# Weight sums for the last down projection moved to GpSimd, in tiles taken from the transfer scratch

## The chip, the cores and the metric

The kernel runs on one core of one Trainium2 chip, as one program from one launch. The metric is the device time of that program in microseconds (us); smaller is better. Engines carry the profile's names: PE is TensorE, PEld its weight loads, DVE is VectorE, ACT is ScalarE, POOL is GpSimd and SP is SyncE, which here only issues transfers. SPq, ACTq and POOLq are the queues from which an engine issues transfers (DMAs).

## What is computed

Two layers of a decoder trunk over 512 positions of width 1024, all float32. A layer is a mixer and a gated MLP, each with a norm ahead of it and a residual sum behind it:

```
for l in range(2):
    h = rmsnorm(x, norm1_g[l]);  p = h @ w_in[l]
    y_rw  = rwkv7_branch(...)        # 8 heads of 64, state recurrence over the positions
    y_ret = retention_branch(...)    # 4 heads, chunks of 128 positions
    y_sg  = sgu_branch(...)          # gated spatial unit, chunks of 128
    gates = sigmoid(gate_logits)
    x = x + (sum over the 3 branches of gates * (y @ w_branch)) @ w_out[l]
    u = rmsnorm(x, norm2_g[l]) @ ffn_w_up[l]         # 1024 -> 2 x 2816
    c = causal convolution of width 3 over the positions of u
    x = x + (silu(gate half of c) * value half of c) @ ffn_w_down[l]   # 2816 -> 1024
return rmsnorm(x, final_g)
```

## The kernel before

All products are made on TensorE in three passes: each operand is split into a rounded part and a remainder (`hi`, `lo`), and `mm3` (L152, the matmul itself at L156) issues three products (hi by lo, hi by hi, lo by hi) of mostly 128 x 128 by 128 x 512. Weights come as 128 x 512 units: `load` issues the transfer from SP into a raw tile `wr`, `part` makes the rounded part on ACT (L139, tiles `wh` or `sh`) and the remainder on DVE (L140, `wl` or `sl`). The program is built twice; the first pass notes the order of the units, the second fetches ahead by that plan (`unit`, `AHEAD`). The order of the instructions on each engine is set when the program is built, by a scheduler that goes by priority (program order, if nothing else is said) and by a modelled time; `keep_in_program_order` pins an instruction behind whatever its engine has traced before it. On the chip each engine then runs its queue strictly in order.

Tiles of 128 x 512 float32 (2 KiB per partition) come from rotating pools: `u` has `NU` = 31, `r` has 16, `f` (while the merges and the MLP run) has 39. A tile is given again when its last reader is done.

One layer runs so. `rwkv`: columns of the projection, `prep` per pair of heads (ends with four masks on POOL, L579 and L580), then `solve`, a triangular solve on DVE that begins with copies of diagonal blocks (L769 on ACT, L771 on POOL), then the recurrence over eight chunks of 64 positions. In the solve and the recurrence, TensorE fills its waits with `fill`: columns of the gates, retention and spatial unit, kept in store by the generator `fillers`. A chunk passes from the state S (L712, L713 on DVE) to XB (L687 on DVE) to U (L701 on ACT) and back, each time with small products at L664. Every second chunk ends with a power operation on POOL (L732). Behind the recurrence come `sgu_v` (power operation L990), and the merges in the order written out in `SEQ`: S stands for a row of retention (power operation L961 on POOL), 0, 2 and 1 for a branch's merge of one column block. A merge fetches its gate (`gth`, L1034, POOL queue), multiplies on DVE (L1037) and adds on POOL or DVE (L1040). Then `wout`, `ffn_up`, and `ffn_down` in the first layer, `last` in the second.

`last` makes the last down projection in a form with fewer products: of each pair of row blocks of the weight it uses four tiles as they are and four sums or differences of them. The sums do not depend on data, and the kernel makes them ahead and puts them into DRAM (`tsum`), from where `last` fetches them like weights (`ts` tiles, SP queue). There are eleven pairs q, each with four loads, four sums and four stores. In the kernel before, all of that is done in the first layer's MLP by `presum`, which is called in `ffn_up` and `ffn_down` where the table `PRE` says so: loads and stores from the POOL queue, sums on DVE (L242 to L245), in tiles of the pools `f` (`fpre`, sixteen tiles) and `u`.

Of the kernel before, what the change touches and what calls it, by code (L numbers as in the profile page):

```python
# [8 lines left out]
F32 = mybir.dt.float32  # L9
# [6 lines left out]
L = 2  # L16
# [3 lines left out]
NFF = 22  # L20
DFF = 2816
RWC, RETC, SGC = 1792, 1536, 1024
NU, NR, NFP = 31, 16, 39
FILL = (36, 2, 1)
KEPT = 6
PRE = {(0, "f", 2): 0, (0, "f", 4): 1, (0, "f", 6): 2, (0, "f", 8): 3, (0, "d", 0): 4, (0, "d", 1): 5, (0, "d", 2): 6, (0, "d", 3): 7,
       (0, "d", 4): 8, (0, "d", 5): 9, (0, "d", 6): 10}
# [24 lines left out]
class Emit:  # L52
    def __init__(self, ctx, tc, a, plan=None):

        self.plan, self.used = plan, []
        self.raws, self.parts, self.nraw, self.npart = [], [], 0, 0
        self.pool, self.fp, self.pin, self.keep, self.turn = None, None, False, False, 4
        self.tc, self.nc, self.a = tc, tc.nc, a
        tp = lambda n, b, **k: ctx.enter_context(tc.tile_pool(name=n, bufs=b, **k))
        self.cp = tp("cp", 1)  # L60
        self.wp = tp("wp", 2)
        self.up = tp("up", NU)
        self.rg = tp("rg", NR)
# [172 lines left out]

    def presum(self, l, stage, m):

        if self.pre:
            q, b = self.pre.pop()  # L240
            V = self.nc.vector
            V.tensor_tensor(b[3], b[3], b[1], op=SUB)  # L242
            V.tensor_tensor(b[1], b[1], b[0], op=SUB)
            V.tensor_tensor(b[0], b[0], b[3], op=ADD)
            V.tensor_tensor(b[2], b[2], b[0], op=SUB)  # L245
            for p, t in zip((7, 5, 6, 4), (b[3], b[1], b[0], b[2])):
                self.tsum[q, p] = self.dp.tile([128, 512], F32, name=self.nm("ts"))
                self.nc.gpsimd.dma_start(self.tsum[q, p], t)
        q = PRE.get((l, stage, m))
        if q is not None:  # L250
            b = self.fpre.pop(0) if stage == "f" else [self.u(n="pre") for _ in range(4)]
            for i, t in enumerate(b):
                self.nc.gpsimd.dma_start(t, self.a["wdt"][0, 2 * q + i // 2][:, i % 2 * 512:i % 2 * 512 + 512])
            self.pre.append((q, b))

# [68 lines left out]
    def run(self):  # L324
        nc, tc, a, V = self.nc, self.tc, self.a, self.nc.vector
        self.con = self.cp.tile([128, NCC], F32, name="con")
        self.pre, self.tsum = [], {}
        self.rst = self.cp.tile([128, 512], F32, name="rst")
# [132 lines left out]
    def rwkv(self, l, nst):  # L461
# [64 lines left out]
        def prep(m):  # L526
# [146 lines left out]
        for c in range(8):  # L673
# [13 lines left out]
            V.tensor_copy(xb, Q[:, 1])  # L687
            self.fill(FILL[2], True)
            Q = self.sm((128, 2, 4, 64)) if c < 7 else None
            for i in (0, 4, 5, 6, 7, 1, 2, 3):  # L690
                for h in range(2):
# [7 lines left out]
                    else:  # L699
                        mm(P1[hv[o], 0, m, :], Y[m][hv[o], c, 64:128], vop(hv[o], m, c))  # L700
            A.copy(U, P1[:, 1])  # L701
            self.fill(FILL[2], True)
            for m, h in mh:
# [339 lines left out]
    def wout(self, l, mg, xd, st):  # L1043
        nc, V = self.nc, self.nc.vector
        out = []
        for m in range(8):
            xi = self.u(n="xi")
            nc.sync.dma_start(xi, xd[m])
            ps = self.acc()
            self.matF(ps, ("wall", l, 70 + m, 0), mg)  # L1050
            V.scalar_tensor_tensor(xi, ps, 0.5, xi, op0=MUL, op1=ADD)
            out.append(xi)
            self.norm_z(st, xi, "n2")
            self.norm_sq(st, xi)
# [3 lines left out]
    def ffn_up(self, l, st, x):  # L1058
# [9 lines left out]
        first = self.firstF(l, (78, 79, 80), st, (3,))  # L1068
        if l == 0:
            self.fpre = [[self.f(n="pre") for _ in range(4)] for _ in range(4)]  # L1070
        for i in range(NFF):
            if l == 0 and i % 2 == 0 and 2 <= i <= 10:
                self.presum(l, "f", i)
            if x and i % 2 == 1 and i < 17:
# [42 lines left out]
    def ffn_down(self, l, act, x, st):  # L1117
# [3 lines left out]
        for m in range(8):  # L1121
# [7 lines left out]
            xd.append(d)  # L1129
            self.presum(l, "d", m)  # L1130
        return x, xd


    def last(self, act):
# [8 lines left out]
        def unit(p, q):  # L1143
            if p > 3:
                return self.unit("tsum", 0, (q, p), 0)
            return self.unit("wdt", 0, 2 * q + (p > 1), 512 * (p == 3))
# [289 lines left out]
```

## Time and profile before

| | |
|---|---|
| time, median of 3 runs | 1703.91 us (1703.56 to 1705.05) |
| the profiled execution's own time | 1701.58 us |
| its span, first to last instruction | 1699.7 us |
| granted TensorE clock | 0.999 |
| TensorE busy | 1687.0 us (99%) |
| VectorE busy | 1233.1 us (73%) |
| ScalarE busy | 799.9 us (47%) |
| GpSimd busy | 240.8 us (14%) |
| moved by DMA | 260.01 MB, 153 GB/s on the mean |

Busy time is the time in which an engine has an instruction in work; TensorE's matmuls overlap each other, so that a matmul of 128 x 512 shows 390 ns. The stretches of the span are, roughly: to 345 us the first layer's heads and recurrence, to 460 its merges, to 510 its output projection, to 865 its MLP (down projection from 755), to 985 the second layer's head preparation, to 1045 its solve, to 1155 its recurrence, to 1303 gating unit and merges, to 1345 the output projection, to about 1595 the up projection, then `last`.

### The profile page before, as it was taken

Reading aid. Unit: us, or ns where it says so; the run is one execution under the profiler, and the core shown is the slowest. Engines: PE = TensorE matmul, PEld = TensorE weight load, DVE = VectorE, ACT = ScalarE, POOL = GpSimd, SP = SyncE. Lnnn points to the kernel's source line nnn. Section 1 sums busy time; section 2 is a strip of 40 time slices with the busy share of each in tenths; the row PEclk is TensorE's granted clock in tenths of the full one; section 3 lists DMA queues with packets and bytes.
Section 4 is the critical chain, followed back from the end, with each engine's and each line's share of the span. In section 5 each row is a group of like instructions: output and inputs, shape, how many; then the busy total and the mean of one; then the engine's idle time right before and its main releaser. Section 6 shows DMA issues by size and latency. Waiting matters only on the chain.

```text
span 1699.7 us, 27885 instructions
## 1 busy us (share of the span) xinstructions
PE 1687.0 (99%) x10214; PEld 1379.7 (81%) x10214; DVE 1233.1 (73%) x2157; ACT 799.9 (47%) x1367; POOL 240.8 (14%) x336
## 2 busy tenths in 40 slices
PE   9999999999999999999999999999999999999998
PEld 7888777888888888888888888777888888887786
DVE  6887746578669887655568888455775698888776
ACT  6563433554355444433355644335542554444565
POOL 2121000003301200003321210000132022110000
PEclk9999999999999999999999999999999999999999
DMA  5236552524544532147743365525254443433774
GB/s 182 87 108 203 177 179 94 181 92 161 189 146 147 194 123 95 63 145 260 255 142 100 97 211 172 180 94 188 85 173 149 155 136 132 130 131 112 241 243 167
DMA packets 147768, 260.01 MB, mean 153 GB/s; under 512 B 19600, under 2 KB 39952, under 8 KB 147632
## 3 DMA queue, kind: packets, MB, share of 16 engines
q1 hardware_dynamic: 122960, 192.87, 35.2%
q0 software_dynamic: 15888, 49.95, 8.7%
q10 hardware_dynamic: 8784, 15.42, 2.6%
q8 instruction: 80, 1.31, 0.3%
q14 instruction: 56, 0.46, 0.1%
HBM read 212.94 MB, written 45.22 MB: 152 GB/s over the span
## 4 chain that ended last, share of the span: by engine, by line
PE 90%; DVE 4%; DMA 3%; issue 1%; ACT 1%; SPq 0%; ACTq 0%; DVEq 0%
PE acc L156 82%; PE sm L156 3%; PE sm L664 2%; DVE wl L140 1%; DMA wr<-wall 1%; PE sm L917 1%; PE sm L571 1%; DMA tr<-bkT 1%; DVE sl L140 0%; PE sm L1022 0%; ACT wh L139 0%; DVE cs L790 0%; DMA wr<-ts 0%; DVE TMP L788 0%; DMA x<-xT 0%
## 5 line engine op out<-in xcount | busy, mean ns | idle before, releaser
L156 PE MATMUL acc<-lo,sh 128*128 128x512 f32 x1108 | 431.8, 390 | 0.5 <-ACT sh L139 0.5
L156 PE MATMUL acc<-hi,sh 128*128 128x512 f32 x1108 | 431.9, 390 | 0.0
L156 PE MATMUL acc<-hi,sl 128*128 128x512 f32 x1108 | 430.3, 390 | 0.2 <-DVE sl L140 0.2
L139 ACT CAST sh<-wr 128x512 fp32r<-128x512 f32 (+1 forms) x375 | 228.3, 615 | 370.3 <-PE acc L156 217.6
L140 DVE TENSOR_TENSOR sl<-wr,sh 128x512 fp32r<-128x512 f32 (+1 forms) x375 | 254.5, 684 | 103.5 <-ACT sh L139 78.3
L140 DVE TENSOR_TENSOR wl<-wr,wh 128x512 fp32r<-128x512 f32 x238 | 166.5, 703 | 144.5 <-ACT wh L139 141.1
L139 ACT CAST wh<-wr 128x512 fp32r<-128x512 f32 x238 | 146.8, 619 | 244.4 <-PE acc L156 160.3
L156 PEld LDWEIGHTS acc<-lo,sh 128*128 128x128 f32 x1108 | 208.0, 188 | 45.0 <-ACT sh L139 1.2
L156 PEld LDWEIGHTS acc<-hi,sl 128*128 128x128 f32 x1108 | 208.0, 188 | 44.1 <-DVE sl L140 0.7
L156 PEld LDWEIGHTS acc<-hi,sh 128*128 128x128 f32 x1108 | 208.0, 188 | 43.1 <-issue 0.3
L156 PE MATMUL acc<-lo,wh 128*128 128x512 f32 x588 | 232.3, 395 | 0.3 <-DVE lo L215 0.2
L156 PE MATMUL acc<-hi,wl 128*128 128x512 f32 x588 | 229.8, 391 | 0.5 <-DVE wl L140 0.5
L156 PE MATMUL acc<-hi,wh 128*128 128x512 f32 x588 | 229.3, 390 | 0.0
L156 PEld LDWEIGHTS acc<-lo,wh 128*128 128x128 f32 x588 | 110.5, 188 | 25.5 <-DVE lo L215 1.5
L156 PEld LDWEIGHTS acc<-hi,wl 128*128 128x128 f32 x588 | 110.4, 188 | 25.4 <-DVE wl L140 1.5
L156 PEld LDWEIGHTS acc<-hi,wh 128*128 128x128 f32 x588 | 110.6, 188 | 22.5 <-issue 0.2
L156 PE MATMUL acc<-ah,sh 128*128 128x512 f32 x352 | 108.4, 389 | 0.0
L1084 ACT ACTIVATE cv<-fu,pc 128x512 f32<-128x512 f32 x88 | 71.6, 816 | 61.1 <-DVE fu L1082 59.8
L1082 DVE TENSOR_TENSOR fu<-acc,rsF 128x512 f32<-128x512 f32 x88 | 60.6, 688 | 39.8 <-PE acc L156 39.7
L156 PE MATMUL acc<-wl,hi 128*128 128x512 f32 x212 | 86.1, 406 | 0.0
L156 PE MATMUL acc<-wh,lo 128*128 128x512 f32 x212 | 82.8, 391 | 0.0
L156 PE MATMUL acc<-wh,hi 128*128 128x512 f32 x212 | 82.7, 390 | 0.0
(359 smaller groups left out, 2426.8 us busy)
## 6 DMA issues: line engine op xcount, KB each, us to landing
wr<-wall SPq DMA_DIRECT2D x488, 256.0 KB, 2.8
gd<-gth ACTq DMA_DIRECT2D x48, 256.0 KB, 3.0
gth<-gd POOLq DMA_DIRECT2D x48, 256.0 KB, 3.5
pre<-wdt POOLq DMA_DIRECT2D x44, 256.0 KB, 5.9
ts<-pre POOLq DMA_DIRECT2D x44, 256.0 KB, 2.8
wr<-ts SPq DMA_DIRECT2D x44, 256.0 KB, 3.9
wr<-wdn SPq DMA_DIRECT2D x40, 256.0 KB, 4.2
wr<-wdt SPq DMA_DIRECT2D x33, 256.0 KB, 3.6
```

What stands on the lines that cost most here:

```text
L139: self.kept(self.nc.scalar.copy(hi[:, :n], raw[:, :n]))
L140: self.kept(self.nc.vector.tensor_tensor(lo[:, :n], raw[:, :n], hi[:, :n], op=SUB))
L156: i = self.nc.tensor.matmul(*x, **y, **kw)
L571: i = T.matmul(pK[hv[1 - h], j, :], bk[hv[h], c, 1, :], x[hv[h], c, :], start=True, stop=True)
L664: po(T.matmul(o, l, r, start=start, stop=True, skip_group_check=True))
L917: po(T.matmul(X[h][:, i, :], lhsT, rhs, start=new[h], stop=stop, skip_group_check=True))
L1082: V.tensor_tensor(u, ps, self.rsF, op=MUL)
L1084: A.activation(t, u, AF.Identity, scale=self.p("cw2", j), bias=self.p("cb", j))
```

## The change

The sums move from DVE in the first layer's MLP to POOL in the second layer's mixer. The generator `sums` holds their steps: four loads into a pool `pp` of four tiles of its own, then an empty step, then four steps of one sum and one store, then an empty one; all of them are POOL instructions and pinned in program order. `presum` now takes a step of it. It is called twice at the end of each `prep` (four times), three times in each chunk (eight), behind each step of the gating unit (nine), ahead of each step of `SEQ` (33) and in each column block of `wout` (eight): 82 calls for 77 steps, in the second layer only (in the first the generator is empty). The room for the tiles comes from the scratch that the program keeps for POOL's transfers, which is set to 4096 bytes per partition (`dynamic_dma_scratch_size`); six tiles are added, four in `pp` and two in `u` (`NU` 33). The tables and the sixteen `fpre` tiles of the first layer go.

```diff
-NU, NR, NFP = 31, 16, 39
+NU, NR, NFP = 33, 16, 39
-PRE = {(0, "f", 2): 0, (0, "f", 4): 1, ... (0, "d", 6): 10}
+RING = 4096
...
+        self.pp = tp("pp", 4)
...
-        src = self.tsum[i] if name == "tsum" else self.a[name][l, i]
+        src = self.tsum[(l, *i)] if name == "tsum" else self.a[name][l, i]
...
-    def presum(self, l, stage, m):
-        if self.pre:
-            q, b = self.pre.pop()
-            V = self.nc.vector
-            V.tensor_tensor(b[3], b[3], b[1], op=SUB)
-            V.tensor_tensor(b[1], b[1], b[0], op=SUB)
-            V.tensor_tensor(b[0], b[0], b[3], op=ADD)
-            V.tensor_tensor(b[2], b[2], b[0], op=SUB)
-            for p, t in zip((7, 5, 6, 4), (b[3], b[1], b[0], b[2])):
-                self.tsum[q, p] = self.dp.tile([128, 512], F32, name=self.nm("ts"))
-                self.nc.gpsimd.dma_start(self.tsum[q, p], t)
-        q = PRE.get((l, stage, m))
-        if q is not None:
-            b = self.fpre.pop(0) if stage == "f" else [self.u(n="pre") for _ in range(4)]
+    def sums(self, l):
+        P, po = self.nc.gpsimd, self.tc.keep_in_program_order
+        for q in range(NFF // 2 if l else 0):
+            b = [self.pp.tile([128, 512], F32, name=self.nm("pre"), tag="pre") for _ in range(4)]
             for i, t in enumerate(b):
-                self.nc.gpsimd.dma_start(t, self.a["wdt"][0, 2 * q + i // 2][...])
-            self.pre.append((q, b))
+                po(P.dma_start(t, self.a["wdt"][l - 1, 2 * q + i // 2][...]))
+            yield
+            yield
+            for p, o, x, op in ((7, 3, 1, SUB), (5, 1, 0, SUB), (6, 0, 3, ADD), (4, 2, 0, SUB)):
+                po(P.tensor_tensor(b[o], b[o], b[x], op=op))
+                self.tsum[l, q, p] = self.dp.tile([128, 512], F32, name=self.nm("ts"))
+                po(P.dma_start(self.tsum[l, q, p], b[o]))
+                yield
+            yield
+
+    def presum(self, n=1):
+        for _ in range(n):
+            next(self.sum, None)
...
# mixer
-            self.filler = self.fillers(l)
+            self.filler, self.sum = self.fillers(l), self.sums(l)
...
             next(step) if step else self.sgu_bias()
+            self.presum()
...
         for step in SEQ.split():
+            self.presum()
...
# rwkv, end of prep
             X.append(x); Y.append(y); BK.append(bk)
+            self.presum(2)
...
# rwkv, in each chunk: behind the tile of P1, behind XB, behind U
+            self.presum()
...
# wout, in each column block
+            self.presum()
...
# ffn_up and ffn_down: the calls of presum and the tiles fpre are gone
...
-        nc = _bacc.Bacc("TRN2", target_bir_lowering=False, num_devices=1)
+        nc = _bacc.Bacc("TRN2", target_bir_lowering=False, num_devices=1, dynamic_dma_scratch_size=RING)
```

More of the change, by code (lines that the diff above doesn't have):

```diff
@@ L235, in trip @@
         return d
-    def presum(self, l, stage, m):
-        if self.pre:
-            q, b = self.pre.pop()
-            V = self.nc.vector
-            V.tensor_tensor(b[3], b[3], b[1], op=SUB)
-            V.tensor_tensor(b[1], b[1], b[0], op=SUB)
-            V.tensor_tensor(b[0], b[0], b[3], op=ADD)
-            V.tensor_tensor(b[2], b[2], b[0], op=SUB)
-            for p, t in zip((7, 5, 6, 4), (b[3], b[1], b[0], b[2])):
-                self.tsum[q, p] = self.dp.tile([128, 512], F32, name=self.nm("ts"))
-                self.nc.gpsimd.dma_start(self.tsum[q, p], t)
-        q = PRE.get((l, stage, m))
-        if q is not None:
-            b = self.fpre.pop(0) if stage == "f" else [self.u(n="pre") for _ in range(4)]
-            for i, t in enumerate(b):
-                self.nc.gpsimd.dma_start(t, self.a["wdt"][0, 2 * q + i // 2][:, i % 2 * 512:i % 2 * 512 + 512])
-            self.pre.append((q, b))
+    def sums(self, l):
+        P, po = self.nc.gpsimd, self.tc.keep_in_program_order
+        for q in range(NFF // 2 if l else 0):
+            b = [self.pp.tile([128, 512], F32, name=self.nm("pre"), tag="pre") for _ in range(4)]
+            for i, t in enumerate(b):
+                po(P.dma_start(t, self.a["wdt"][l - 1, 2 * q + i // 2][:, i % 2 * 512:i % 2 * 512 + 512]))
+            yield
[9 more added lines that the diff above has]
+            next(self.sum, None)
     def norm_new(self):
@@ L326, in run @@
         self.con = self.cp.tile([128, NCC], F32, name="con")
-        self.pre, self.tsum = [], {}
+        self.tsum = {}
         self.rst = self.cp.tile([128, 512], F32, name="rst")
@@ L701, in rwkv @@
             A.copy(U, P1[:, 1])
+            self.presum()
             self.fill(FILL[2], True)
@@ L1052, in wout @@
             out.append(xi)
+            self.presum()
             self.norm_z(st, xi, "n2")
@@ L1068, in ffn_up @@
         first = self.firstF(l, (78, 79, 80), st, (3,))
-        if l == 0:
-            self.fpre = [[self.f(n="pre") for _ in range(4)] for _ in range(4)]
         for i in range(NFF):
-            if l == 0 and i % 2 == 0 and 2 <= i <= 10:
-                self.presum(l, "f", i)
             if x and i % 2 == 1 and i < 17:
@@ L1129, in ffn_down @@
             xd.append(d)
-            self.presum(l, "d", m)
         return x, xd
@@ L1144, in unit @@
             if p > 3:
-                return self.unit("tsum", 0, (q, p), 0)
+                return self.unit("tsum", L - 1, (q, p), 0)
             return self.unit("wdt", 0, 2 * q + (p > 1), 512 * (p == 3))
```

2 lines of the change are left out of this document (removed).

## The prediction

> **What bounds the kernel now.** I read the page first, then busy time by stage (stretches cut by hand), then the waits of TensorE, then the order of time around the moved work.
>
> ```profile
> span 1699.7 us, 27885 instructions
> ```
>
> ```profile
> 510.00:755.00 245.00, 245.00 (x1082) 202.93 (x1082) 197.54 (x311) 114.27 (x179) 15.15 (x29) 1.00 0.37 123
> 755.00:865.00 110.00, 110.00 (x487) 91.10 (x486) 59.04 (x93) 34.15 (x60) 34.23 (x64) 1.00 0.75 251
> ...
> 1045.00:1150.00 105.00, 104.78 (x1559) 81.75 (x1559) 55.61 (x110) 45.19 (x89) 7.15 (x7) 1.00 0.45 143
> ```
>
> The columns of a stretch are its length, then busy time of TensorE, its weight loads, VectorE, ScalarE and GpSimd, the granted clock, the DMA share and GB/s. The first two stretches are the first layer's gated MLP (up, then down projection), where all the removed work stands: TensorE is busy 245.00 of 245.00 us and 110.00 of 110.00. The third is the second layer's recurrence, where the products are small and TensorE is busy 104.78 of 105.00 us. TensorE is the bound in all three, at a full clock, and another engine matters only where it makes TensorE stand still.
>
> ```profile
> PE acc L156 <- DVE sl L140: 0.7, 1, 0.7
> ```
>
> ```profile
> 1175.00:1190.00 15.00, 14.29 (x63) 11.18 (x62) 8.87 (x14) 9.61 (x16) 0.00 (x0) 1.00 0.47 161
> 1550.00:1575.00 25.00, 24.27 (x106) 19.32 (x105) 19.44 (x33) 9.76 (x16) 1.62 (x3) 1.00 0.34 111
> 1575.00:1600.00 25.00, 24.40 (x105) 19.25 (x104) 20.14 (x34) 13.04 (x23) 2.70 (x5) 1.00 0.63 193
> ...
> 1655.00:1690.00 35.00, 34.66 (x153) 28.40 (x152) 28.47 (x52) 19.83 (x41) 2.17 (x4) 1.00 0.56 188
> 1690.00:1700.00 10.00, 2.48 (x11) 1.71 (x10) 2.81 (x7) 3.13 (x9) 0.00 (x0) 0.82 0.29 105
> ```
>
> The first row heads TensorE's waits between 1045 and 1345 us: one wait of 0.7 us. The next four rows are the places behind the first layer where it loses time that more tiles or a freer VectorE could give back: 0.71 + 0.73 + 0.60 + 0.34 = 2.4 us in all. The last row is the tail, 7.5 us without products.
>
> **What is removed.**
>
> ```profile
> L242 DVE TENSOR_TENSOR pre<-pre,pre 128x512 f32<-128x512 f32 x11 | 7.6, 690 | 15.8 <-DMA pre<-wdt 15.8
> ...
> L245 DVE TENSOR_TENSOR pre<-pre,pre 128x512 f32<-128x512 f32 x11 | 7.5, 686 | 0.0
> ```
>
> These are the first and the last of four groups: 44 VectorE operations of some 0.69 us, 30 us of VectorE, and 15.8 us in which it stood waiting for their data. With them 44 loads and 44 stores leave the GpSimd queue of the first layer, 23 MB that made part of the 251 GB/s of its down projection, and the 16 "pre" tiles leave the big pool. All of it lay beside a TensorE without a gap, so it gives back 0. If that cover were missing, at most 30 + 16 us could come back; the two full stretches exclude it.
>
> **What is added.** The same 44 sums on GpSimd, in the second layer between its per-head preparation and its output projection, four tiles at a time: each group is four loads, an empty step, then four times a sum and its store. By the calls in the code that is 4 sums in the preparation, 14 in the recurrence, 6 in the gating unit, 20 in the merges and the output projection.
>
> ```profile
> L248 POOL DMA_DIRECT2D ts<-pre x44 | 23.9, 542 | 194.8 <-DVE pre L242 169.3 <-DVE pre L245 8.4 <-DVE pre L243 6.0
> L253 POOL DMA_DIRECT2D pre<-wdt x44 | 23.4, 539 | 0.0
> L1040 POOL TENSOR_TENSOR gth<-gth,gth 128x512 f32<-128x512 f32 x16 | 21.4, 1338 | 65.0 <-DVE gth L1037 65.0
> ```
>
> A sum of this shape takes GpSimd 1.3 us (the merges' adds), an issue 0.54. So GpSimd gets 44 x 1.3 + 88 x 0.54 = 57 + 48 = 105 us more, over some 400 us; in the recurrence it is busy 7.15 of 105.00 us now. Its own time is no term. What can cost is what stands behind it.
>
> First, the queue. The new instructions are pinned behind whatever GpSimd has traced, so the loads after the last head's masks stand in front of the diagonal copies that start the triangular solve.
>
> ```profile
> 984.20 2.58 POOL L771 COPY cs<-GB 32x1024 f32<-32x1024 f32 x2
> ```
>
> ```profile
> 1037.76 2.28 DVE L794 STREAM_TRANSPOSE cs<-cs 128x512 f32<-128x512 f32 x2
> ```
>
> ```profile
> 1045.38 1.34 PE L808 MATMUL sm<-cs,GB 32*32 32x32 f32 x128
> ```
>
> Four issues put 2.2 us in front of the copies; the solve ends on VectorE at 1040.04 and its first product runs at 1045.38, behind filler products. Slack 5.3 us, price 0; without the fillers it would be 2.2. A sum whose loads have not landed makes GpSimd's small power operations (L732, L961, L990) and the gate loads behind it wait, and VectorE, in order, for those. The landing of the present loads and stores together is 2.3 to 7.7 us, median 4.5, and the code leaves one step between:
>
> ```profile
> DMA to landing us min/median/max: 2.3/4.5/7.7
> ```
>
> ```profile
> ACT sh L139 <- PE acc L156: 37.5, 19, 4.4
> ```
>
> The second view (waits, 1045 to 1345 us) says that ScalarE's weight casts wait mostly for TensorE to free tiles: weights are ready ahead, so a late VectorE does not starve TensorE at once. I take 0.5 us for the gating unit and the merges together, between 0 and 3.8 (five retention rows at 0.75, the overshoot worked out below).
>
> Second, VectorE itself.
>
> ```profile
> 428.29 1.29 POOL L1040 TENSOR_TENSOR gth<-gth,gth 128x512 f32<-128x512 f32 x1 [3.11 <-DVE gth L1037]
> ```
>
> ```profile
> 427.52 1.29 DVE L1037 SCALAR_TENSOR_TENSOR gth<-gth,acc 128x512 f32<-128x512 f32 x2
> ```
>
> ```profile
> 453.47 1.28 POOL L1040 TENSOR_TENSOR gth<-gth,gth 128x512 f32<-128x512 f32 x1 [3.78 <-DVE gth L1037]
> ```
>
> ```profile
> 454.15 1.15 DVE L140 TENSOR_TENSOR sl<-wr,sh 128x512 fp32r<-128x512 f32 x1 [0.77 <-ACT sh L139]
> ```
>
> Beside a GpSimd add that ends at 454.75, the weight remainder L140, which reads two SBUF tiles like the removed sums and at their 0.69 us when undisturbed, takes 1.15 and ends 0.55 behind the add. Two L1037, with one operand in PSUM, run at full speed beside another add (0.65 each). So a VectorE operation with two SBUF operands waits for the end of a running GpSimd sum, 1.29 us at most. That is what the Trainium skill says (SBUF — State Buffer, SBUF: two separate sides): the shared port pair is held exclusively for a whole instruction, by a GpSimd operation or a two-SBUF-input VectorE one, and the loser blocks. It speaks against this change, and by it alone 44 sums would hold VectorE off for up to 57 us. The trace agrees in the rows above. What matters is where VectorE has no 1.3 us to spare, and that is the recurrence.
>
> ```profile
> 1101.29 0.69 DVE L140 TENSOR_TENSOR wl<-wr,wh 128x512 fp32r<-128x512 f32 x1 [3.32 <-ACT wh L139]
> 1101.90 0.42 DVE L712 TENSOR_TENSOR S<-S,sm 128x256 f32<-128x256 f32 x1
> 1102.35 0.42 DVE L713 TENSOR_TENSOR S<-S,F 128x256 f32<-128x256 f32 x1
> ...
> 1105.67 0.68 DVE L140 TENSOR_TENSOR wl<-wr,wh 128x512 fp32r<-128x512 f32 x1
> 1106.27 0.42 DVE L687 COPY XB<-sm 128x256 f32<-128x256 f32 x1
> ```
>
> ```profile
> 1104.18 0.62 PE sm L664 x32
> ...
> 1107.75 1.09 PE sm L664 x64
> ```
>
> The state S is done at 1102.77 and TensorE reads it at 1104.18: slack 1.41 us. XB is done at 1106.69 and read at 1107.75: slack 1.06. One blocked operation costs at most 1.29: S still fits, XB is 0.23 late. Two blocked in a row (L140, then L713 behind a second sum that started beside L712: 1.29 + 1.29 - 0.42 = 2.16) make S 0.75 late. Of the 14 sums here I let 4 meet such a step, at about 0.3 us each, nearer to the single hit of 0.23 than to the double one: +1.2, between 0 and 14 x 0.75 = 10.5. In the preparation TensorE loses nothing measurable now; I take 0 for 4 sums, at most 4 x 0.75 = 3.
>
> **Two more u tiles, four tiles of their own, the smaller scratch.** More u tiles can only give back stalls; I take 0.5 of the 2.4 us. No row shows the scratch. If it is large enough for what is in flight, it costs 0; the row nearest to a queue that holds back is a landing of 4.5 us instead of an issue of 0.54. I take 0, since at most a dozen transfers are issued within one landing.
>
> **Sum.** 0 + 1.2 + 0.5 - 0.5 = +1.2 us. The profiled execution took 1701.58 us (span 1699.7 and 1.9 around it), so it would be 1702.8; the three timed runs have a median of 1703.91, 2.3 above the profiled one, so I forecast 1705.1 there.
>
> **Rivals.**
> *The held port costs the recurrence (slower).* The sums come in bursts right behind a power operation or a landing, and two in a row beat S by 0.75 us. If half of the 14 hit so, it is +5.3 us, with the merges' 3.8 at worst +9.1: 1709 to 1713. It decides from five such hits on. For it: the slack rows; L140 stands before S and XB in order. Against: a sum needs its load, and the loads come only every seventh step.
> *More tiles close the gaps (faster).* All four gaps of 2.4 us vanish and nothing else costs: 1701.5. Reaching beyond 0.2% needs 3.4 us, so a changed order would have to shorten the tail of 7.5 us too. For it: VectorE is 78% busy just before the gaps of 1550 to 1600. Against: the sums are not there in either version.
> *The scratch holds GpSimd's queue (slower).* If transfers wait for earlier ones to land, the MLP's stores "ab" come late, and VectorE overwrites what they read. Eleven pairs at the shortest landing, 2.3 us, make 25 us of VectorE, of which its idle 22 per cent there (25.00 less 19.44, from 1550 on) covers most; a tenth to a quarter left over is +2.5 to +6, 1706 to 1710. For it: these stores are issued from the same queue. Against: the code has eight GpSimd transfers per pair there, which is few.
>
> **How the numbers follow.** About 0.2%, 3.4 us, is what a measurement of this kernel tells from no change. Forecast (stalls of a few tenths, within 0.2%) 0.50; the held port beyond 3.4 us 0.30; the scratch or a less fortunate order of the schedule beyond 3.4 us 0.10; gaps closed beyond 3.4 us 0.10. So faster 0.10, same 0.50, slower 0.40. The range goes from all gaps closed, with half a microsecond of spread, to the held port near its full price: 1701.0 to 1712.0. The forecast's own range is 1702 to 1707.
>
> **What would show it.** Right: both first-layer MLP stretches as full and as long as before; GpSimd some 105 us busier, all between 900 and 1330 us; L140 and L713 of the second recurrence longer or later by up to 1.3 us where a sum runs; 0 to 2 us more idle TensorE in 1045 to 1150. Wrong: a first-layer MLP that gets shorter; TensorE waiting on S, XB or a power operation for over 3.4 us in all; GpSimd issues of far over 0.54 us, which would be the scratch; or the stalls of 1550 to 1600 us gone together with a shorter tail.

## The result, and the profile after

The changed kernel takes 1741.37 us (median of 4 runs, 1740.48 to 1747.11) against 1703.74 us for the kernel before in the same comparison (1703.07 to 1705.05): a ratio of 1.0227, with a 95% interval of 1.0204 to 1.0250, so some 38 us more. The forecast was 1705.1 us with a range to 1712.0. The profiled execution took 1740.48 us.

Of the page of the kernel after, the span, the busy time of the engines, and GpSimd's three new groups (lines behind the recurrence stand seven lower than before: L1037 is now L1044, L1040 L1047, L713 L720, L664 L668; L139, L140 and L156 are unchanged):

```profile
span 1738.7 us, 27762 instructions
...
PE 1702.8 (98%) x10214; PEld 1385.9 (80%) x10214; DVE 1248.0 (72%) x2113; ACT 800.0 (46%) x1367; POOL 302.4 (17%) x380
```

```profile
L247 POOL TENSOR_TENSOR pre<-pre,pre 128x512 f32<-128x512 f32 x44 | 60.6, 1377 | 19.9 <-DMA pre<-wdt 19.1
...
L249 POOL DMA_DIRECT2D ts<-pre x44 | 24.8, 564 | 9.5 <-POOL pre L247 9.5
L243 POOL DMA_DIRECT2D pre<-wdt x44 | 23.9, 547 | 13.2 <-DMA ts<-pre 12.7 <-issue 0.5
```

GpSimd does what the change says: 60.6 + 24.8 + 23.9 = 109 us of new work. VectorE lost 30 us of sums and is nevertheless 15 us busier (1248.0 after 1233.1): most of the 45 us between is time in which its instructions stood still (below).

Busy time by stretch of the kernel after, in the columns of before (length, TensorE, its weight loads, VectorE, ScalarE, GpSimd, clock, DMA share, GB/s); the last fence is the stretch of the kernel before that answers to the last row:

```profile
510.00:755.00 245.00, 245.00 (x1082) 203.00 (x1081) 188.53 (x296) 115.15 (x179) 0.00 (x0) 1.00 0.29 93
755.00:865.00 110.00, 110.00 (x487) 91.11 (x486) 42.14 (x67) 35.02 (x59) 4.33 (x8) 1.00 0.40 117
...
1045.00:1150.00 105.00, 101.48 (x1469) 79.35 (x1468) 65.81 (x113) 43.17 (x83) 39.62 (x45) 0.98 0.58 187
...
1243.00:1345.00 102.00, 86.98 (x396) 69.06 (x395) 77.69 (x106) 29.98 (x56) 65.15 (x80) 0.92 0.65 214
```

```profile
1230.00:1310.00 80.00, 80.00 (x412) 66.60 (x411) 59.82 (x105) 29.00 (x52) 26.55 (x33) 1.00 0.52 171
```

The first layer's MLP is as full as before. In the merges with the output projection 102 us hold 396 products, where 80 us held 412 before; TensorE idles 15 of the 102 us, at a mean clock of 0.92. To see where the delay arises I compare the start of the n-th product of TensorE (10214 are recorded in every trace) with that of before. It grows by

| kernel | 0 to 865 (times of before) | preparation, to 1000 | solve, first chunks, to 1100 | recurrence, gating unit, to 1225 | merges, output projection, to 1345 | behind, to 1680 |
|---|---|---|---|---|---|---|
| after | 1.1 | 4.2 | 2.9 | 4.3 | 26.3 | -0.4 |
| transfers only (e2) | 0.8 | 1.5 | 4.8 | 6.2 | 12.9 | -0.1 |
| sums only (e3) | 1.7 | 2.1 | 2.4 | 7.2 | 9.5 | -0.2 |
| a quarter of the bytes (x3) | 1.1 | 0.3 | 2.7 | 0.2 | 10.2 | 0.1 |
| tiny transfers (y1) | 0.5 | 0.2 | 1.5 | 0.3 | 10.1 | 0.1 |
| tiny sums (y2) | 1.7 | 0.0 | 0.0 | -0.7 | 2.7 | -0.7 |

in us, from one profiled execution each. The lower rows belong to the experiments. Differences of 1 to 2 us are common among kernels that share the code of a stage (first column). Cut at the borders of the stages instead, the kernel after loses 2.1 us in the preparation (865 to 985), 3.8 in the solve (to 1045), 5.3 in the recurrence (to 1150), 0.1 in the gating unit (to 1230) and 25.6 in the merges (to 1303).

TensorE's waits between 865 and 1345 us; before, the list had one wait of 0.7 us and one of 0.2 us:

```profile
PE acc L156 <- DVE gth L1044: 9.8, 5, 2.6
PE sm L924 <- DVE sc L945: 4.5, 3, 2.0
PE sm L668 <- DVE S L720: 2.5, 1, 2.5
```

TensorE waits for VectorE's multiplies that empty a result bank in the merges, for the retention's score tiles, and once for the state S.

The order of time in the output of the merges, VectorE first and GpSimd below (start, duration):

```profile
1302.82 3.89 DVE L140 TENSOR_TENSOR sl<-wr,sh 128x512 fp32r<-128x512 f32 x1 [0.16 <-ACT sh L139]
1306.63 1.77 DVE L1047 TENSOR_TENSOR gth<-gth,gth 128x512 f32<-128x512 f32 x1
```

```profile
1301.77 1.31 POOL L247 TENSOR_TENSOR pre<-pre,pre 128x512 f32<-128x512 f32 x1
1303.02 1.30 POOL L1047 TENSOR_TENSOR gth<-gth,gth 128x512 f32<-128x512 f32 x1
1304.25 0.57 POOL L249 DMA_DIRECT2D ts<-pre  x1
1304.84 1.31 POOL L247 TENSOR_TENSOR pre<-pre,pre 128x512 f32<-128x512 f32 x1
1306.08 1.10 POOL L1041 DMA_DIRECT2D gth<-gd  x2
```

A weight remainder of 0.69 us takes 3.89: it starts beside a sum, and is done 0.56 us after the end of the *third* GpSimd operation (1304.84 + 1.31 = 1306.15). At the two ends in between, GpSimd went on (at the second with the issue of a store) and VectorE did not get its turn. The longest hold is in the retention, where four operations that take 1.13 us undisturbed take 6.94 beside sums and adds:

```profile
1272.04 1.13 DVE L971 SCALAR_TENSOR_TENSOR vt<-ry,rrr,vt 128x128 f32<-128x128 f32 x4
...
1277.49 6.94 DVE L971 SCALAR_TENSOR_TENSOR vt<-ry,rrr,vt 128x128 f32<-128x128 f32 x4
```

Summed over 865 to 1345 us, VectorE's instructions run 45.9 us beyond the lower quartile of their own line and shape (counting those over by more than 0.15 us); before, 7.6 us in the same stages.

Not every wait of the merges is a hold. Of the five waits on L1044, two (4.8 us, ending at 1312.65 and 1336.86) come behind VectorE operations that were held. Two (4.1 us, ending at 1292.22 and 1321.91) come after VectorE itself stood still, with the multiply queued behind a remainder that waits for a cast:

```profile
1290.88 0.69 DVE L140 TENSOR_TENSOR sl<-wr,sh 128x512 fp32r<-128x512 f32 x1 [2.25 <-ACT sh L139]
...
1320.47 0.69 DVE L140 TENSOR_TENSOR sl<-wr,sh 128x512 fp32r<-128x512 f32 x1 [2.62 <-ACT sh L139]
```

The fifth (0.9 us) waits for a gate that has not landed.

### The profile page after: what moved, and what is told of

It reads as the page before. It is cut to its first block, busy times and chain, and to the rows that moved or that the text cites. A ratio compares the mean times of both kernels' runs of the same rounds, so it can differ in the third digit from the quotient of the medians.

```text
span 1738.7 us, 27762 instructions
## 1 busy us (share of the span) xinstructions
PE 1702.8 (98%) x10214; PEld 1385.9 (80%) x10214; DVE 1248.0 (72%) x2113; ACT 800.0 (46%) x1367; POOL 302.4 (17%) x380
## 3 DMA queue, kind: packets, MB, share of 16 engines
q8 instruction: 80, 1.31, 0.3%
## 4 chain that ended last, share of the span: by engine, by line
PE 70%; DMA 9%; DVE 9%; issue 7%; ACT 2%; SPq 2%; POOL 1%; ACTq 0%; POOLq 0%; DVEq 0%
PE acc L156 63%; DMA wr<-wall 4%; PE sm L156 3%; DVE wl L140 2%; PE sm L668 2%; DMA tr<-bkT 1%; SPq L625 1%; DVE sl L140 1%; SPq L230 1%; DMA tr<-yt 1%; PE sm L924 1%; ACT wh L139 1%; DMA ws<-sgw 1%; DMA tr<-qkt 1%; ACT sh L139 1%
## 5 line engine op out<-in xcount | busy, mean ns | idle before, releaser
L156 PE MATMUL acc<-lo,sh 128*128 128x512 f32 x1108 | 435.6, 394 | 10.5 <-DVE gth L1044 10.0
L156 PE MATMUL acc<-hi,sh 128*128 128x512 f32 x1108 | 434.7, 392 | 0.0
L156 PE MATMUL acc<-hi,sl 128*128 128x512 f32 x1108 | 433.5, 393 | 0.2 <-DVE sl L140 0.2
L139 ACT CAST sh<-wr 128x512 fp32r<-128x512 f32 (+1 forms) x375 | 228.2, 615 | 359.0 <-PE acc L156 265.5
L140 DVE TENSOR_TENSOR sl<-wr,sh 128x512 fp32r<-128x512 f32 (+1 forms) x375 | 263.7, 708 | 141.0 <-ACT sh L139 79.5
L140 DVE TENSOR_TENSOR wl<-wr,wh 128x512 fp32r<-128x512 f32 x238 | 174.1, 734 | 144.7 <-ACT wh L139 141.9
L139 ACT CAST wh<-wr 128x512 fp32r<-128x512 f32 x238 | 146.8, 619 | 242.0 <-PE acc L156 142.8
L156 PEld LDWEIGHTS acc<-lo,sh 128*128 128x128 f32 x1108 | 209.6, 189 | 57.6 <-issue 8.5
L156 PEld LDWEIGHTS acc<-hi,sl 128*128 128x128 f32 x1108 | 209.7, 189 | 45.1 <-DVE sl L140 0.7
L156 PEld LDWEIGHTS acc<-hi,sh 128*128 128x128 f32 x1108 | 209.9, 189 | 43.7 <-issue 0.3
L156 PE MATMUL acc<-lo,wh 128*128 128x512 f32 x588 | 232.8, 396 | 1.7 <-ACT wh L139 1.5
L156 PE MATMUL acc<-hi,wl 128*128 128x512 f32 x588 | 230.5, 392 | 0.8 <-DVE wl L140 0.8
L156 PE MATMUL acc<-hi,wh 128*128 128x512 f32 x588 | 229.5, 390 | 0.0
L156 PEld LDWEIGHTS acc<-lo,wh 128*128 128x128 f32 x588 | 110.5, 188 | 28.0 <-ACT wh L139 3.5
L156 PEld LDWEIGHTS acc<-hi,wl 128*128 128x128 f32 x588 | 110.4, 188 | 27.5 <-DVE wl L140 3.8
L156 PEld LDWEIGHTS acc<-hi,wh 128*128 128x128 f32 x588 | 110.6, 188 | 22.2 <-issue 0.2
L156 PE MATMUL acc<-ah,sh 128*128 128x512 f32 x352 | 108.4, 389 | 0.0
L156 PE MATMUL acc<-wl,hi 128*128 128x512 f32 x212 | 86.9, 410 | 0.0
L156 PE MATMUL acc<-wh,lo 128*128 128x512 f32 x212 | 83.5, 394 | 0.0
L156 PE MATMUL acc<-wh,hi 128*128 128x512 f32 x212 | 83.4, 393 | 0.0
```

Source lines behind the costliest of these rows:

```text
L139: self.kept(self.nc.scalar.copy(hi[:, :n], raw[:, :n]))
L140: self.kept(self.nc.vector.tensor_tensor(lo[:, :n], raw[:, :n], hi[:, :n], op=SUB))
L156: i = self.nc.tensor.matmul(*x, **y, **kw)
```

## The experiments

Theories: H, the GpSimd sums hold VectorE off; T, the 88 transfers cost it, by their bytes (C), by what waits in GpSimd's queue (Q), or by the order that the schedule builds around them (O); S, the scratch or the tiles. All ratios are to the kernel before, run in the same comparison.

**Scratch and tiles (e1), and five raw tiles as well (x4).**

```diff
# kernel before
+RING = 4096        # and dynamic_dma_scratch_size=RING
-NU, NR, NFP = 31, 16, 39
+NU, NR, NFP = 33, 16, 39          # x4: 31, and NRAW = 5 for 3
```

> The kernel before with only the scratch of 4096 bytes and NU 33; sums as before on VectorE in the first layer. Theory H (GpSimd's sums hold VectorE off the shared port) and theory T (the 88 transfers inside the second mixer collide with its own): 1702 to 1705 us, as before. Theory S (the smaller scratch or the changed tiles cost it): 1715 us or more, with GpSimd issues far over 0.55 us.

> The kernel before with the small scratch and five raw weight tiles, NU 31: a control for the raw tiles. All theories: 1701 to 1706 us, since nothing waits for weights before.

e1 took 1703.18 us, 1.0007 (0.9997 to 1.0016); x4 1704.43 us, 0.9998 (0.9989 to 1.0007). GpSimd's issues last as long as before in e1 (543 ns for the stores, 542 before). S is out, and two more tiles give back nothing.

**The two halves of the change (e2, e3).**

```diff
# e2, kernel after
-                po(P.tensor_tensor(b[o], b[o], b[x], op=op))
# e3, kernel after: tiles, loads and stores for q == 0 alone
+                if q:
+                    self.tsum[l, q, p] = self.tsum[l, 0, p]
```

> The kernel after without its 44 sums: the loads and stores stay at their steps (the stored tiles are then the plain weights; the sums are left out). H: the +25 us of merges and output projection goes, and most of the +6 of preparation and solve; what stays is the late weight transfer in the recurrence at some 1100 us, +4: 1706 to 1711 us. T: 1732 to 1741 us.

> The kernel after with loads and stores of the first pair alone: the other 40 sums run at their steps on the same four tiles and nothing waits for a landing (the sums of the other pairs are left out). H: 1728 to 1737 us, with VectorE's two-operand work held by some 35 us between 865 and 1345 us as in the kernel after. T: 1704 to 1708 us.

e2 took 1725.48 us, 1.0140 (1.0110 to 1.0170), and e3 1722.00 us, 1.0108 (1.0091 to 1.0125): 24 and 18 us, which together make 42, about the 38 of the change. Both lie between what the two theories expected, so neither has it alone. In e3 VectorE is held 50.8 us by the sum above, in e2 10.1.

**What a sum costs by: its time (y2), and its length (e4).**

```diff
# y2, kernel of e3                                # e4, kernel after
-    po(P.tensor_tensor(b[o], b[o], b[x], op=op))
+    po(P.tensor_tensor(b[o][:, :8], b[o][:, :8], b[x][:, :8], op=op))       # y2
+    for k in range(0, 512, 128):                                            # e4: four of 128 columns
+        po(P.tensor_tensor(b[o][:, k:k + 128], b[o][:, k:k + 128], b[x][:, k:k + 128], op=op))
```

> The sums without further transfers, each of 8 columns instead of 512: the same 44 instructions at the same steps, some 0.1 us each (the sums are left out). H (the time for which a sum holds the port): 1703 to 1706 us. O (GpSimd's order and what the schedule builds around it): 1714 to 1722 us, as with whole sums.

> The kernel after with each sum cut into four GpSimd operations of 128 columns, some 0.4 us each. If VectorE gets the port at the end of the running GpSimd operation, as the prediction had it, a hit costs at most 0.4 instead of 1.3 us: 1712 to 1722 us. If VectorE stays off while GpSimd goes from one operation straight to the next, the cut changes nothing or costs the four starts: 1740 to 1752 us. T: 1738 to 1745 us.

y2 took 1703.76 us, 1.0014 (1.0005 to 1.0024): the same 44 instructions at the same steps cost 2 us instead of 18 when they are short, and VectorE's held time is 8.8 us, near the 7.6 of before. The other ways in which a long sum could cost time are small here: VectorE's queue in y2 differs from that in e3 in 11 of 2113 places, and in e3 the engines wait 7.5 us for results of GpSimd between 865 and 1345 us, against 6.7 before. This shows H for the sums alone: it is the time for which they hold VectorE off. e4 took 1739.10 us, 1.0215 (1.0199 to 1.0230). VectorE's held time falls from 45.9 to 29.9 us, but the time only from 1.0227 to 1.0215, far from the 1712 to 1722 us that went with a hit of 0.4 us. VectorE gets in between two quarters, though not at the first end; of one remainder beside four quarters:

```profile
1106.11 1.72 DVE L140 TENSOR_TENSOR wl<-wr,wh 128x512 fp32r<-128x512 f32 x1 [2.55 <-ACT wh L139]
```

```profile
1105.97 2.16 POOL L248 TENSOR_TENSOR pre<-pre,pre 128x128 f32<-128x128 f32 x4
```

The remainder is done at 1107.83, inside the four quarters that run from 1105.97 to 1108.13: by the single records the third ends at 1107.26, 0.57 us ahead of that, and the fourth is drawn out from 0.45 to 0.91 us. So a hit is shorter, yet not as short as one quarter. Part of what the shorter holds give back goes into another wait. VectorE's multiplies wait for gates that land late (1200 to 1355 us; in the kernel after 2.4 us, before none), and TensorE's waits for the multiplies grow from 9.8 us to 15.3 (865 to 1345 us):

```profile
DVE gth L1045 <- DMA gth<-gd: 11.7, 6, 5.1
```

```profile
PE acc L156 <- DVE gth L1045: 15.3, 5, 7.0
```

The four gate loads behind the longest of these waits are issued at 1284.51, behind sums, stores and loads that keep GpSimd busy from 1270 on. How much of this is GpSimd's queue and how much the traffic is not separated.

**What a transfer costs by (x3, y1, e7).**

```diff
# x3, y1: kernel of e2 with 32 partitions (x3) or 1 (y1) of each load and store
-                po(P.dma_start(t, self.a["wdt"][l - 1, 2 * q + i // 2][:, ...]))
+                po(P.dma_start(t[:32], self.a["wdt"][l - 1, 2 * q + i // 2][:32, ...]))
# (x3, y1: the last down projection reads plain weights)
# e7: kernel of e2, the stores take a constant tile, made once on GpSimd; NU 32 for its room
-                po(P.dma_start(self.tsum[l, q, p], b[o]))
+                po(P.dma_start(self.tsum[l, q, p], self.zero))
```

> The kernel after without sums, and with stores that take a constant tile instead of the loaded one: the same 44 loads and 44 stores of 256 KB at the same steps, but no instruction of GpSimd waits for a landing (the sums are left out). Theory Q (the queue waits): 1703 to 1709 us. Theory C (the traffic itself makes weights, gates and the transposed tiles land late): 1720 to 1727 us, as with the transfers of the loaded tiles.

> The transfers without sums again, but each load and store of 32 of the 128 partitions, so a quarter of the bytes with the same 88 issues at the same steps (the sums are left out; the last down projection reads plain weights in their place). C: 1704 to 1711 us. If what counts is the number of issues, their places in GpSimd's queue or the changed order of the schedule: 1719 to 1728 us.

> The transfers without sums, each of one partition (2 KB): the same 88 issues at the same steps with next to no bytes (the sums are left out; the last down projection reads plain weights in their place). Full tiles cost 23 us, a quarter 14, of which 10 in merges and output projection. If the bytes do it (C): 1703 to 1707 us. If the 88 issues in GpSimd's queue and the order that the schedule builds around them do it (O): 1711 to 1717 us, with the 10 us still in 1225 to 1345.

e7 took 1741.89 us, 1.0213 (1.0198 to 1.0228), which no theory expected. GpSimd stands 3.5 us ahead of the added issues, against 38 in e2, and the same bytes cost more, not less, so Q falls as the cause of the transfers' 24 us. Of the 42 us by which its profiled execution is longer, 7 arise before 865 us, in code that it shares with the others, and 35 behind; its longest wait is 6.6 us for the state S. Why it loses more than e2 was not followed further. x3 took 1717.26 us, 1.0072 (1.0055 to 1.0089), and y1 1712.31 us, 1.0067 (1.0052 to 1.0082). So some 12 of the 24 us go with the bytes, and some 11 stay with next to none; VectorE's queue in y1 differs from that in e2 in 22 of 2113 places, from that in x3 in 4. x3 fell between its two expectations, y1 where O had it. The table by stages separates them: ahead of the merges e2 loses 12.5 us, x3 3.2 and y1 2.0; in merges and output projection 12.9, 10.2 and 10.1.

The bytes first. A weight's time from issue to landing in the merges, before and after (the last line of the view of the tile wr):

```profile
DMA to landing us min/median/max: 2.2/2.6/5.7
```

```profile
DMA to landing us min/median/max: 2.5/3.8/8.0
```

In the recurrence it is one chain, in e2 as in the kernel after. Before, the state's output y is stored to be transposed, and SyncE, in order, waits for that before it can issue the next weight:

```profile
1087.96 0.33 SPq L234 DMA_DIRECT2D tr<-yt  x1
1094.99 1.75 SPq L230 DMA_DIRECT2D yF<-tr  x4
1096.84 13.37 SPq L126 DMA_DIRECT2D wr<-wall  x6
```

Before, four table loads are issued just ahead of that store. In the kernel after the four loads of a pair stand ahead of them, and the same steps become

```profile
1096.19 0.33 SPq L234 DMA_DIRECT2D tr<-yt  x1
1104.68 3.12 SPq L230 DMA_DIRECT2D yF<-tr  x4
1107.90 10.73 SPq L126 DMA_DIRECT2D wr<-wall  x5
```

with the weight at ScalarE at

```profile
1112.58 0.62 ACT L139 CAST wh<-wr 128x512 fp32r<-128x512 f32 x1 [6.32 <-DMA wr<-wall]
```

VectorE has to make that weight's remainder ahead of S, S comes late, and TensorE waits 2.5 us (the wait on S L720 above). No sum is in this chain: its share is there in e2 (6.2 us) and gone with small transfers (0.2 and 0.3).

**The half without bytes (z1, z2; y3, y4; x2).** In y1 TensorE's list of waits in the merges (1240 to 1320 us) is headed by

```profile
PE acc L156 <- DVE gth L1043: 5.6, 3, 1.9
```

and VectorE's order of time at the first of them is

```profile
1271.34 0.69 DVE L140 TENSOR_TENSOR sl<-wr,sh 128x512 fp32r<-128x512 f32 x1 [1.72 <-ACT sh L139]
1271.94 1.88 DVE L1043 SCALAR_TENSOR_TENSOR gth<-gth,acc 128x512 f32<-128x512 f32 x3
1277.55 0.69 DVE L140 TENSOR_TENSOR sl<-wr,sh 128x512 fp32r<-128x512 f32 x1 [3.73 <-ACT sh L139]
```

Three multiplies, which would free three result banks, stand behind a remainder that waits for a cast, which waits for TensorE to free a weight tile. The order is fixed when the program is built. z1 and z2 pin it:

```diff
# kernel of y1 (z1), kernel after (z2)
                 yret = self.ret_out()
+                self.keep = True          # loads, casts, remainders in program order; off behind SEQ
...
-        nc.vector.scalar_tensor_tensor(t, t, 1.0, ps, op0=ADD, op1=MUL)
+        self.kept(nc.vector.scalar_tensor_tensor(t, t, 1.0, ps, op0=ADD, op1=MUL))
# y3 (kernel after), y4 (kernel of e1), in merge
-        nc.gpsimd.dma_start(t, self.gd[br, m])
+        nc.sync.dma_start(t, self.gd[br, m])
# x2, kernel after
-NU, NR, NFP = 33, 16, 39        -NRAW = 3
+NU, NR, NFP = 31, 16, 39        +NRAW = 5
```

> The run with 88 tiny transfers and no sums, where behind the retention (the last 15 steps of the merges' order, in both layers) the weight loads, casts and remainders and the merges' multiplies are pinned in program order, so that one multiply follows each remainder on VectorE. Theory O (the longer GpSimd queue makes the schedule put multiplies behind remainders that wait for TensorE, and TensorE then waits for a result bank): the 10 us of merges and output projection shrink to 0 to 4, 1702 to 1707 us; the first layer's merges, which have no sums, show what the pins alone do. If the order isn't it: 1710 to 1716 us.

> The kernel after with the same pins. O and H together: the order's 10 us come back and the port's and the bytes' share stay, 1726 to 1734 us. If the order isn't it, or the held port makes up for it: 1737 to 1745 us.

z1 took 1710.93 us, 1.0032 (1.0020 to 1.0044): half of y1's cost is gone. By the start of the products the merges and the output projection lose 4.8 us instead of 10.1, and the first layer's merges, with the same pins and no sums, -0.1. TensorE's list there is now

```profile
PE acc L156 <- ACT sh L139: 3.5, 2, 2.1
PE acc L156 <- DVE sl L140: 0.4, 1, 0.4
```

The waits for the multiplies are gone, so half of the half is shown to be order. The whole time lies in the range that was expected if order were not the cause (1710 to 1716), partly because z1's own solve came out 3 us worse; the gain stands in the merges, where 0 to 4 us were expected to stay. z2 took 1746.22 us, 1.0227 (1.0202 to 1.0252): with whole sums and whole transfers the order gives back nothing. There VectorE's multiplies wait 17.4 us for gates that land late (1200 to 1355 us; 2.4 in the kernel after), which may hide a gain in the order.

> The kernel after with the merges' 24 gate loads of each layer issued from SyncE, past GpSimd's queue. Q (gate loads stand behind sums and stores that wait): 12 to 25 us come back in merges and output projection, 1716 to 1729 us. If the gates are not what is late: 1735 to 1748 us.

> Control: the kernel before with the small scratch and two more u tiles, and the gate loads issued from SyncE. All theories: 1701 to 1708 us; more if SyncE, in order, then holds weights back behind a gate that waits for its tile.

> The kernel after with five raw weight tiles instead of three (NRAW 5) and NU 31, so the same bytes. Theory C (the added traffic makes weights land late and three raw tiles are too few to cover it): some 15 to 25 of the 38 us come back, 1714 to 1726 us. Theory H alone, or a loss through gate loads and queue: 1735 to 1745 us.

y3 took 1737.06 us, 1.0212 (1.0193 to 1.0231), y4 1710.09 us, 1.0056 (1.0038 to 1.0073): moving the gate loads costs 9.5 us by itself in y4, mostly in the first layer's merges and output projection, and in the changed kernel's merges nothing comes back (25 us against 26). That does not clear the gate loads. On SyncE they stand behind weights, and VectorE's multiplies wait 20.3 us for them (2.4 in the kernel after, 1200 to 1355 us), so the gates came late there in another way. The control does not carry over either: before 865 us y4 loses 9.1 us and y3, with the same move, 2.7. x2 took 1735.55 us, 1.0175 (1.0153 to 1.0197): against their own runs of before the median is 6 to 9 us better than that of the kernel after, but its profiled execution loses 36.4 us between 865 and 1345 us against 37.7 (less in the merges and the output projection, 20.0 against 26.3, and more ahead of them), so more raw tiles are not the cure.

**Where the sums stand (e5, e6, e6b, x1).**

```diff
# e5, kernel after: nothing pinned
-        P, po = self.nc.gpsimd, self.tc.keep_in_program_order
+        P, po = self.nc.gpsimd, lambda x: x
# e6: kernel after, SEQ's and wout's calls moved; e6b: all calls moved, presum(4)
         for i in range(NFF):
+            if l:
+                self.presum(2)
# x1, kernel before, in presum
-            V = self.nc.vector
+            V = self.nc.gpsimd
```

> The kernel after without the pins on loads, sums and stores: the schedule may put GpSimd's power operations, gate loads and adds ahead of a sum that still waits. Theory Q (what waits for a landing at the head of GpSimd's queue holds the gate loads and adds behind it, some 20 us of the 38) gives 1718 to 1730 us. Theory H (held port, the other 20) alone: no change, 1737 to 1742. If the schedule's modelled landings are too early, the order comes out nearly the same and so does the time, 1735 to 1742.

> The kernel after with the 36 steps of merges and output projection (20 sums) made in the second layer's up projection, two steps per pair of columns. H and Q: the 26 us of 1225 to 1323 come back, the 12 us ahead of it stay, and up projection, where VectorE is idle 38 of 245 us and little stands behind GpSimd's queue, takes 20 sums of up to 1.3 us for 0 to 4: 1714 to 1720 us. If the loss follows the sums wherever they are: 1730 to 1742.

> The kernel after with all 77 steps in the second layer's up projection, four steps per pair of columns. H: 44 holds of some 0.9 us, 40 us, against 38 us of idle VectorE: 1704 to 1716 us, most of it where VectorE works without a pause. Q: little waits behind GpSimd there, 1703 to 1706. If the loss follows the sums wherever they are: 1735 or more.

> The kernel before with the 44 sums on GpSimd instead of VectorE, at their old places in the first layer's MLP, in the old tiles and with the old scratch. If the loss needs a place where VectorE or the weights have nothing to spare (P): VectorE idles 47 of 245 us in the up projection there and 51 of 110 us in the down projection, which takes 44 holds of about 0.9 us: 1702 to 1708 us. If a sum on GpSimd costs what it cost in the second mixer (20 us for 44) wherever it stands: 1718 to 1728 us.

e5 took 1747.95 us, 1.0247 (1.0222 to 1.0272), but not where it was expected: without pins the schedule moved all 44 sums to the start of the program, 11 to 260 us, and 45 of its 47 us arise there; the second mixer loses 0.6. e6 took 1725.99 us, 1.0126 (1.0111 to 1.0141), 6 us above its range: the merges lose nothing any more and the stages ahead of them still some 12 us, as expected, but the up projection 10.6 instead of 0 to 4. e6b took 1745.90 us, 1.0243 (1.0226 to 1.0259), where the loss follows the work wherever it stands: all of it in the up projection costs some 40 us there. x1 took 1723.51 us, 1.0110 (1.0095 to 1.0126), and its loss splits by place. The schedule moved the first sixteen sums into the first layer's output projection; twenty-four ran in the down projection:

```profile
462.00:528.00 66.00, 53.12 (x222) 41.80 (x221) 42.27 (x47) 23.33 (x40) 36.44 (x44) 0.97 0.62 212
780.00:880.00 100.00, 100.00 (x443) 82.84 (x442) 56.10 (x60) 30.05 (x53) 62.16 (x78) 1.00 0.71 231
```

In the first TensorE stands for 13 us, and the start of the products falls 16 us behind; in the second, with as much GpSimd work and more traffic, it has no gap: VectorE works 56 of 100 us there. The last four sums ran into the second layer's preparation, where another 4 us are lost. In the up projection of e6b VectorE works 87%:

```profile
1350.00:1640.00 290.00, 261.87 (x1099) 210.84 (x1098) 252.76 (x350) 117.09 (x186) 137.46 (x191) 0.95 0.55 183
```

VectorE's idle time alone does not explain x1's output projection, though: before, VectorE was busy only 30.65 of 50.00 us there. TensorE's waits in x1 are for the residual sums L1051, and those wait for a transfer (460 to 530 us):

```profile
PE acc L156 <- DVE xi L1051: 10.1, 5, 3.2
```

```profile
DVE xi L1051 <- DMA xi<-xT: 10.2, 3, 5.4
```

These loads take a median of 6.2 us from issue to landing, 3.3 before, and VectorE waited 4.3 us for them before. In e6b, too, ScalarE's casts wait 44.5 us for weights (1340 to 1640 us), against 10.8 in the up projection before. So the loss by place is one of the port and the transfers together, and no run of this group separates them.

The expectation for x1 (1702 to 1708) missed because the sums did not stay in their place. No variant was faster than the kernel before.

## Why the prediction was wrong

Right: the removal gave back 0, since both stretches of the first layer's MLP stayed full. GpSimd got 109 us for 105. The scratch cost 0. The four issues stood 2.15 us ahead of the diagonal copies.

Wrong in size:

- **Gating unit and merges, +0.5 us (0 to 3.8).** This is the step that failed: it is 26.3 us with the output projection, 25.6 of them in the merges themselves. With the sums alone (e3) these stages lose 9.5 us, with the transfers alone (e2) 12.9. The price rested on two readings. The first was that a hold ends with the running sum, 1.29 us at most; the remainder above took 3.89. The Trainium skill (SBUF — State Buffer, SBUF: two separate sides) says that whoever starts first keeps the shared pair for the whole instruction and the other blocks. The runs bear out the blocking: 3.89 us for 0.69 beside whole sums, and next to no held time beside tiny ones (y2). What the price lacked is that the blocked one can lose again to GpSimd's next instruction. The second was that weights are ready ahead, so that a late VectorE does not starve TensorE. It starves it by another way: the multiplies that free the result banks are in the same queue, and they come late behind held operations, behind a remainder that waits, or for a late gate.
- **The added traffic.** No term and no rival had it. The prediction counted 23 MB out of the first layer's MLP, and never into the second mixer, where e2 shows 24 us for the transfers alone: about half by bytes, half with hardly any.
- **Recurrence, +1.2 (0 to 10.5).** The kernel after loses 5.3 there (1045 to 1150), within the bounds, but by luck: its one long wait is by the late weight, not by a held S or XB. The price for holds was low as well: sums alone lose 4.3 there and 3.8 in the gating unit.
- **Preparation, 0 (at most 3), and the four issues, 0.** Preparation lost 2.1, within its bound, and the solve 3.8. The tiny transfers (y1) have the same four issues and lose nothing in the solve; whole ones (e2) 4.8.
- **More tiles, -0.5.** Nothing (e1).

The rival of the held port had the right mechanism at 5 to 9 us, but put most of it into the recurrence; with the tiny sums as measure it is worth some 16 to 18 alone, more than half of it behind the recurrence. The rival of the scratch is refuted. A hint stood in the trace of before: VectorE was busy 59.82 of 80.00 us in the merges and 59.04 of 110.00 in the down projection. The prediction read its stretches for TensorE only.

What stays open: a quarter of the transfers' cost (about 5 us in z1's merges), why e7 loses more than e2, and how the late gates of e4, y3 and z2 divide between the queue and the traffic. The two costs, 18 and 24 us alone, do not simply add.

## What to carry to other kernels

Work that is free where it stands is free because of that place's slack in *every* resource it touches; ask for each (here VectorE's port, the transfers, the order of the queues) what the new place has left, and split the change into its halves before believing a sum of small terms. A GpSimd operation with SBUF operands can be paid by VectorE, so an idle GpSimd is no sign that a stage has room. The one stage here that took the work without a gap (x1, down projection) had VectorE busy 56%, but such a figure alone does not tell: in the output projection the transfers landed late. An instruction that cannot cost anything by its own time can still move the order that a scheduler builds, so compare the queues, not only the waits.

## What the runs showed of the hardware

A VectorE operation with two SBUF operands can be held through several GpSimd operations in a row (3.89 us for 0.69), and between shorter ones (0.45 us) it got in only after the third, taking 1.72. By the recorded starts the first to start does not always win: the L971 row above starts at 1277.49, while a store's issue runs on GpSimd and ahead of the sum of

```profile
1277.75 1.30 POOL L247 TENSOR_TENSOR pre<-pre,pre 128x512 f32<-128x512 f32 x1
```

and its first operation, of 0.34 us, still takes 4.78. Whether the recorded start is the moment at which the operands are first read, the trace does not show.

A stall of 2 to 3 us can cost more than itself. Stretches of 4 us in the kernel after, behind the gap of 2.56 us between product starts that ends at 1292.22:

```profile
1292.00:1296.00 4.00, 3.78 (x12) 2.97 (x13) 2.36 (x5) 0.00 (x0) 1.05 (x1) 0.70 0.79 310
1296.00:1300.00 4.00, 4.00 (x17) 3.28 (x16) 2.11 (x3) 1.84 (x3) 2.24 (x5) 0.87 0.52 150
1300.00:1304.00 4.00, 4.00 (x20) 3.30 (x19) 3.79 (x4) 0.64 (x2) 3.68 (x4) 1.00 0.68 247
```

The granted clock is 0.70, then 0.87, then 1.00: from 1293.8 to 1296.8 us products start every 427 ns instead of every 227. Pauses of 2.42, 2.58 and 3.01 us between product starts were followed by such a stretch as well, one of 2.33 us (ending at 1321.91) was not. In the merges and the output projection of the kernel after these slow products add some 7 us to the 15 of idle time. The Trainium skill (TensorE: Matmul & The Clock Gate, HAM oscillation — how this bites in real kernels) puts the limit for such a fall at idle gaps over some 3.4 us; here a gap of 2.56 us was enough.
